# Hybrid decoder block: the last two experts' rows gathered, normed and stored by index

## Chip, core and metric

One core of one Trainium2 chip runs the whole block in one launch. The metric is device time in microseconds (us). TensorE is called PE, VectorE DVE, ScalarE ACT, GpSimd POOL; SP is the queue that issues plain DMAs.

## What is computed

One decoder layer on 1024 tokens of width 1024: a mixer of two attention groups, then a mixture of 32 experts with two experts for each token, then a last RMSNorm. Only the end matters here:

```python
g_sel = jnp.argmax(g_logits, axis=-1)                  # one group of 8 experts
top_v, top_i = lax.top_k(e_logits, 2)                  # two experts in it
w_top = jax.nn.softmax(top_v, axis=-1) * p_group[:, None]
a = jax.nn.silu(hg) * hu * comb[:, :, None]            # comb: w_top at the token's experts, else 0
y = jnp.einsum('nef,efd->nd', a, w_down)
x = x + gate_f * y
out = rms_norm(x, g_final)
```

## The kernel before

Up to the router all tokens are worked on in eight tiles of 128. The normed rows go to `h2d` and the residual rows to `x2d`, both in DRAM. `tab` holds for each expert a column of up to 128 token numbers; unused places hold numbers beyond the last token, which an indirect DMA skips.

The loop `for e in range(NE)` then takes one expert a turn, in a pipeline that spreads each expert over three turns. `gather(e)` (POOL, indirect DMA) brings the expert's token rows from `h2d` into `xg0` or `xg1`. `tokens_T` transposes them on PE, `tokens` splits them into a high and a low part, `gate_up` multiplies them with the gate and up weights (24 matmuls), `act` makes the gated product, `act_T` and `act_split` turn and split it, and `down_proj` multiplies it with the down weights (10 matmuls). `store` scales the result with the adaLN gate (`y = p * gf` on DVE), and `scatter` adds it by an indirect DMA with addition (POOL) to the rows of `x2d`. Each scatter waits for the one before it. `split_gu` and `split_dn` make the high and low parts of the weights on ACT and DVE, and SP loads weights into a ring of 29 buffers.

The last expert, 31, is not added in full by a scatter. `where(31)`, called in the turn of expert 29, builds one-hot matrices `ow` for the first four tiles, and two index columns, `late` and `early`. In the last turn `store(30)` scatters the rows of expert 30, `fetch(0)` to `fetch(3)` read back the first four tiles of `x2d` (SP), and after `down_proj(31)` `store(31)` scatters the rows of the later tiles alone; `fetch(4)` to `fetch(7)` wait for that. `add_last(i)` adds expert 31 to tile `i` of the first four by one-hot matmuls into `pf` and a DVE add into `xf`.

Each tile then goes through `square` (ACT, sum of squares; for tiles 0, 2 and 4 POOL multiplies the row with the final gain `bfin`), `mean` (DVE, then a square root on ACT), `roots` (four small DVE operations) and `last_norm` (ACT for tiles 0, 2, 4; DVE for the others), whose result SP stores with a plain DMA.

After that stands an `If` that is taken only when an expert has more than 128 tokens. In the runs shown it is not taken.

Order: instructions wrapped in `ko`, and all matmuls and transposes, keep their program order on their engine. The lines that the prediction's steps touch: L71 and L76 (all matmuls and transposes are recorded there), L1539 and L1540 (splits), L1584 and L1586 (`act`), L1599 to L1601 (`act_split`), L1617 (`scatter`), L1623 (`y`), L1641 to L1652 (`where`), L1674 (`fetch`), L1684 (`add_last`), L1689 and L1691 (`square`), L1694 and L1695 (`mean`), L1700 to L1703 (`roots`), L1709 to L1712 (`last_norm` and its store), L1761 (`bfin`), L1766 (table load), L1801 and L1940 (the `If` and the end of the program).

Of the kernel before, what the change touches and what calls it, by code (L numbers as in the profile page):

```python
# [19 lines left out]
NT = 8  # L20
# [18 lines left out]
def hymba_block(ctx: ExitStack, tc: tile.TileContext, x, c, w_ada, b_ada, g_mix, w_in, b_forget,  # L39
# [1510 lines left out]
    def split_dn(e):  # L1550

        hi, lo = fix("wd0h"), fix("wd0l")
        both(hi, lo, raw[e][4])
        DN[e] = hi, lo, raw[e][5]
# [41 lines left out]
    def act_split(e):  # L1596
        p = AS[e]
        hl, af = half("ahl", F32R, (128, 2, 128)), fix("af", F32, (128, 2, 128))[:, e % 2]
# [5 lines left out]
    def down_proj(e):  # L1604
# [15 lines left out]
    def store(e):  # L1620
# [3 lines left out]
        if e < NE - 1:  # L1624
            ko(scatter(e))
        else:
            d = ko(scatter(e, OW["late"]))
            for i in range(EARLY):
                tc.declare_no_dep(d.ins, XL[i].ins, reason="rows of later tiles")
# [7 lines left out]
    def where(e):  # L1637

        tn, fn = sm("tn", [128, EARLY + 1], bufs=1), sm("fn", [128, 2], bufs=1)
        ow = OW[e] = u("ow", F32R, (128, EARLY * 128))  # L1640
        ko(V.tensor_copy(tn[:, 0:1], tab[:, e:e + 1]))  # L1641
        for i in range(EARLY):
            ko(V.tensor_scalar(tn[:, i + 1:i + 2], tn[:, 0:1], -128.0 * i, None, op0=OP.add))
        for i in range(EARLY):
            ko(V.tensor_scalar(ow[:, i * 128:(i + 1) * 128], places, tn[:, i + 1:i + 2], None, op0=OP.is_equal))
        tn = tn[:, 0:1]

        for j, (name, op) in enumerate((("late", OP.is_lt), ("early", OP.is_ge))):
            ko(V.tensor_scalar(fn[:, j:j + 1], tn, EARLY * 128 - 0.5, float(FAR), op0=op, op1=OP.mult))
            ko(V.tensor_tensor(fn[:, j:j + 1], fn[:, j:j + 1], tn, op=OP.add))  # L1650
            OW[name] = sm(name, [128, 1], I32, bufs=1)
            ko(V.tensor_copy(OW[name], fn[:, j:j + 1]))  # L1652
# [15 lines left out]
    YS, OW, X2, XL, O = [{} for _ in range(5)]  # L1668
    EARLY = 4
    sqf, vf, yf, nf = (const.tile([128, NT], F32, name=n) for n in ("sqf", "vf", "yf", "nf"))  # L1670

    def fetch(i):
        X2[i] = u("xf")
        XL[i] = Q.dma_start(X2[i], x2d[i * 128:(i + 1) * 128])  # L1674

    def add_last(i):

        e = NE - 1
        p = ps2("pf")
        for hf in range(2):  # L1680
            sl = slice(hf * 512, (hf + 1) * 512)
            for a in range(2):
                mm(p[:, sl], OW[e][:, i * 128:(i + 1) * 128], YS[e][a][:, sl], start=(a == 0), stop=(a == 1))
        ko(V.tensor_tensor(X2[i], X2[i], p, op=OP.add))  # L1684
        square(i)
# [19 lines left out]
    POOL = (0, 2, 4)  # L1705

    def last_norm(i, pool=POOL):
# [4 lines left out]
        Q.dma_start(dap(out, i * 128 * D, [[D, 128], [1, D]]), O[i])  # L1712
# [6 lines left out]
    for e in range(NE):  # L1719
# [12 lines left out]
        if e == NE - 3:  # L1732
            where(NE - 1)
        if last:
            down_proj(e - 1)
# [5 lines left out]
        else:  # L1741
            store(e - 1)
            for i in range(EARLY):
                fetch(i)
            split_dn(e)
        act(e)
        if not last:
# [6 lines left out]
        else:  # L1754
            bfin = u("bfin")
            for hf in range(2):
                p = ps1("pbf")
# [187 lines left out]
```

## Time and profile before

| | us |
|---|---|
| three runs, median (lowest to highest) | 1187.88 (1185.55 to 1189.18) |
| profiled execution, its own time | 1188.36 |
| its span, first to last instruction | 1186.6 |
| PE busy in the span | 1059.7 |
| DVE busy | 873.4 |
| ACT busy | 708.1 |
| POOL busy | 251.7 |

Times in the rows are microseconds from the start of the span. A row of a timeline gives start, length, engine, line, operation, and output<-input; in brackets, how long the engine stood idle before it and what ended that. SPq and POOLq are the queues' own instructions. PEclk is the clock that PE was granted, as a share of the full one.

### The profile page before, as it was taken

To read this page: it belongs to the slowest core of one execution; us is meant where nothing else is said; L and a number is where in the kernel's file an instruction comes from. 1 tells how busy PE (TensorE), PEld (TensorE's weight loads), DVE (VectorE), ACT (ScalarE), POOL (GpSimd) and SP (SyncE) were. 2 spreads that over 40 slices of the span, in tenths; PEclk is the share of its full clock that TensorE was granted. 3 is DMA by queue.
4 is the path that set the end of the run, shared out by engine and by line. 5 is a ranking of instruction groups with operands and counts; after the bars stand their busy time and mean duration, and the time that the engine had idled before them with its cause. 6 is when DMAs were issued, how large, how long until landed. Compare 5 with 4: busy or idle time off the path is not lost.

```text
span 1186.6 us, 15360 instructions
## 1 busy us (share of the span) xinstructions
PE 1059.7 (89%) x4983; PEld 798.3 (67%) x4983; DVE 873.4 (74%) x1740; ACT 708.1 (60%) x1247; POOL 251.7 (21%) x240
## 2 busy tenths in 40 slices
PE   2899999999888999988989999975999999989882
PEld 2788998887665655655656678864777777766651
DVE  5846476768865689656478664796999999978856
ACT  7746578876657654644554631334777777756635
POOL 2110210000301111122212122552222223333213
PEclk9799999999889999999999999996999999989996
DMA  9500112323553343635336643766999999999946
GB/s 375 156 18 1 54 54 89 143 86 110 156 165 91 81 99 78 173 104 173 116 83 204 231 139 120 256 250 221 319 339 320 311 323 312 327 306 321 319 135 256
DMA packets 91415, 219.94 MB, mean 185 GB/s; under 512 B 30517, under 2 KB 40933, under 8 KB 91329
## 3 DMA queue, kind: packets, MB, share of 16 engines
q1 hardware_dynamic: 75520, 185.20, 46.3%
q0 software_dynamic: 15808, 33.69, 10.4%
q8 instruction: 42, 0.69, 0.2%
q14 instruction: 45, 0.36, 0.1%
HBM read 192.43 MB, written 42.99 MB: 198 GB/s over the span
## 4 chain that ended last, share of the span: by engine, by line
PE 60%; DVE 15%; DMA 14%; ACT 5%; issue 4%; SPq 1%; POOL 0%; DVEq 0%; ACTq 0%; POOLq 0%
PE pgu L71 10%; PE pp L305 9%; PE py L71 6%; PE pst L71 6%; PE po L71 5%; PE pout L71 5%; PE pvv L451 4%; DMA raw<-in_w_gate_dram 4%; DMA raw<-in_w_down_dram 3%; DMA qx<-mr 3%; PE pmax L71 3%; PE pxt L76 2%; PE pq L71 1%; PE pp L71 1%; DMA x<-in_x_dram 1%
## 5 line engine op out<-in xcount | busy, mean ns | idle before, releaser
L71 PE MATMUL po<-P,VT 128*128 128x512 f32 (+3 forms) x384 | 151.2, 507 | 0.3 <-ACT P L840 0.3
L840 ACT ACTIVATE P<-pst 128x512 f32<-128x512 f32 x192 | 90.8, 488 | 95.0 <-PE pst L71 93.1
L71 PE MATMUL pst<-qx,kx 128*128 128x512 f32 x192 | 97.2, 507 | 17.3 <-DMA qx<-mr 13.4
L1617 POOL DMA_INDIRECT x2d<-y,tab x31 | 58.5, 1887 | 200.1 <-DMA x2d<-y,tab 38.6
L805 DVE TENSOR_REDUCE mx<-pmax 128x1 f32<-128x128 f32 (+3 forms) x80 | 52.7, 673 | 48.0 <-PE pmax L71 47.8
L71 PEld LDWEIGHTS po<-P,VT 128*128 128x128 f32 x384 | 67.6, 199 | 18.6 <-issue 10.4
L71 PE MATMUL py<-raw,af 128*128 128x512 f32 x128 | 69.0, 621 | 11.4 <-DMA raw<-in_w_down_dram 11.3
L71 PE MATMUL pmax<-kx,qx 128*128 128x512 f32 (+1 forms) x192 | 70.4, 431 | 6.4 <-DMA kx<-KB 4.2
L71 PE MATMUL py<-wd0h,ahl 128*128 128x512 f32 x128 | 68.0, 531 | 2.4 <-ACT wd0h L1539 1.9
L71 PE MATMUL pst<-qy,ky 128*128 128x512 f32 x192 | 68.7, 358 | 0.0
L71 PEld LDWEIGHTS pst<-qx,kx 128*128 128x128 f32 x192 | 39.4, 205 | 39.3 <-issue 21.1
L802 DVE CUSTOM_DVE_ANT_0 mjunk<-pmax,madd 128x384 bf16<-128x384 f32 (+5 forms) x48 | 42.6, 888 | 21.9 <-PE pmax L71 21.7
L507 ACT ACTIVATE sjunk<-score,low,sga 128x768 bf16<-128x768 uint16 (+2 forms) x51 | 57.7, 1132 | 1.7 <-DVE low L537 0.8
L507 ACT ACTIVATE sjunk<-k,low 128x768 bf16<-128x768 uint16 (+2 forms) x48 | 49.9, 1039 | 13.3 <-DVE low L537 11.6
L402 DVE SCALAR_TENSOR_TENSOR score<-relu,iw,score 128x384 f32<-128x384 f32 (+5 forms) x42 | 41.0, 976 | 22.6 <-ACT relu L397 19.0
L71 PE MATMUL pout<-woh,oh 128*128 128x512 f32 x128 | 52.0, 406 | 2.4 <-DVE ssq L918 2.4
L71 PE MATMUL pout<-woh,ol 128*128 128x512 f32 x128 | 50.8, 397 | 0.0
L71 PE MATMUL pout<-wol,oh 128*128 128x512 f32 x128 | 50.5, 395 | 0.0
L305 PE MATMUL pp<-hh,wbl 128*128 128x512 f32 x128 | 49.8, 389 | 0.0
L305 PE MATMUL pp<-hl,wbh 128*128 128x512 f32 x128 | 49.8, 389 | 0.0
L305 PE MATMUL pp<-hh,wbh 128*128 128x512 f32 x128 | 49.8, 389 | 0.0
L1540 DVE TENSOR_TENSOR wgu2l<-raw,wgu2h 128x512 fp32r<-128x512 f32 x64 | 43.8, 684 | 8.0 <-ACT wgu2h L1539 8.0
(456 smaller groups left out, 3193.0 us busy)
## 6 DMA issues: line engine op xcount, KB each, us to landing
raw<-in_w_gate_dram SPq DMA_DIRECT2D x64, 512.0 KB
raw<-in_w_up_dram SPq DMA_DIRECT2D x64, 512.0 KB
raw<-in_w_down_dram SPq DMA_DIRECT2D x64, 512.0 KB
wada<-in_w_ada_dram POOLq DMA_DIRECT2D x32, 512.0 KB, 5.5
x<-in_x_dram SPq DMA_DIRECT2D x16, 512.0 KB
wada<-in_w_ada_dram SPq DMA_DIRECT2D x16, 512.0 KB
wbr<-in_w_in_dram SPq DMA_DIRECT2D x8, 512.0 KB
qy<-QB SPq DMA_DIRECT2D x16, 256.0 KB
```

Source lines behind the costliest of these rows:

```text
L71: i = tc.keep_in_program_order(T.matmul(*a, **k))
L76: i = tc.keep_in_program_order(T.transpose(*a))
L305: at["mm"] = (op or T.matmul)(p[:, :n], w(k, a), hT[b][k][:, n0:n0 + n], start=(i == 0), stop=(i == 23))
L402: last = V.scalar_tensor_tensor(score[i], r, wv, score[i], op0=OP.mult, op1=OP.add)
L451: at["mm"] = T.matmul(p[:, :ng], hT[a][k][:, t * 128:(t + 1) * 128], parts[k // kk][b][:, k % kk, :], start=(i == 0), stop=(i == 23))
L507: paced(S.activation(sjunk[:, :(i + 1) * 128], src, AF.Sign, bias=self.col(self.low, i), scale=scale, accum_out=self.col(self.cnt, i)))
L802: V.tensor_tensor_reduce(mjunk[:, :w_], p[:, :w_], madd[i], 1.0, NEG, OP.add, OP.max, accum_out=mx[0][:, i:i + 1])
L805: V.tensor_reduce(mx[0][:, i:i + 1], p[:, :w_], AX.X, OP.max)
L840: S.activation(P[hf, kb][0], p[:, :m], AF.Exp)
L1540: ko(V.tensor_tensor(lo, w, hi.bitcast(F32), op=OP.subtract))
L1617: return G.indirect_dma_start(out=x2d, out_offset=bass.IndirectOffsetOnAxis(ap=at_, axis=0), in_=y, in_offset=None, bounds_check=L - 1, oo ...
```

## The change

Experts 30 (`EA`) and 31 (`EB`) are no longer scattered into `x2d`. When the scatter of expert 29 has landed, `own_rows` gathers the residual rows of their tokens from `x2d` into `xg0` and `xg1`, and all eight tiles are fetched, without these two experts. The rows of expert 30 get its result, those of expert 31 get its own. A token that has both appears in both; `shares()` builds a 128x128 match `MT["m"]` between the two lists, and four more matmuls add expert 30's rows to those of 31, whose copy is the one stored. The gathered rows are treated as tiles 8 and 9 of the norm. Tiles 0 to 5 are stored plainly, also where a token's row lacks one of the two experts. Tiles 7 and 6 are stored by index without the tokens of either expert, then tile 9, and tile 8 without the tokens that tile 9 has. In the last turn, down projection of 30 moves behind gate and up of 31 and the gain; expert 31 gets buffers of its own for its down weights and its product. POOL multiplies for tile 6 too.

```diff
     def split_dn(e):
-        hi, lo = fix("wd0h"), fix("wd0l")
+        hi, lo = (fix(f"wd0{n}") if e < EB else u(f"wd1{n}", F32R) for n in "hl")
...
-            mm(p[:, sl], af, w1[:, sl], start=False, stop=True)
+            mm(p[:, sl], af, w1[:, sl], start=False, stop=(e != EB))
+        if e == EB:
+            for hf in range(2):
+                sl = slice(hf * 512, (hf + 1) * 512)
+                for k in range(2):
+                    mm(p[:, sl], MT["m"], YS[EA][k][:, sl], start=False, stop=(k == 1))
...
-        if e < NE - 1:
+        if e < EA:
             ko(scatter(e))
-        else:
-            d = ko(scatter(e, OW["late"]))
...
+        if e == EA:
             yh, yl = u("yh", F32R), u("yl", F32R)
-            for hf in range(2):
-                sl = slice(hf * 512, (hf + 1) * 512)
-                ko(S.activation(yh[:, sl], y[:, sl], AF.Copy))
-                ko(V.tensor_sub(yl[:, sl], y[:, sl], yh[:, sl].bitcast(F32)))
+            ko(S.activation(yh, p, AF.Copy))
+            ko(V.tensor_sub(yl, p, yh.bitcast(F32)))
             YS[e] = yh, yl
+        if e >= EA:
+            X2[NT + e - EA] = x = xgs[e % 2].bitcast(F32)
+            ko(V.tensor_tensor(x, x, y, op=OP.add))
+
+    def own_rows(e):
+        return ko(G.indirect_dma_start(out=xgs[e % 2], out_offset=None, in_=x2d,
+                                       in_offset=bass.IndirectOffsetOnAxis(ap=tab[:, e:e + 1], axis=0),
+                                       bounds_check=L - 1, oob_is_err=False))
+
+    def shares():
+        tn, fl = sm("tn", [128, 2], bufs=1), sm("fl", [128, 1 + NT], bufs=1)
+        ko(V.tensor_copy(tn, tab[:, EA:EA + 2]))
+        p = ps1("ptn")
+        mm(p[:, 0:128], tn[:, 1:2].to_broadcast([128, 128]), identf, start=True, stop=True)
+        MT["m"] = u("mt", F32R, (128, 128))
+        ko(V.tensor_scalar(MT["m"], p[:, 0:128], tn[:, 0:1], None, op0=OP.is_equal))
+        ko(V.tensor_reduce(fl[:, 0:1], MT["m"].bitcast(F32), AX.X, OP.max))
+        MT["a"] = sm("oa", [128, 1], I32, bufs=1)
+        ko(V.scalar_tensor_tensor(MT["a"], fl[:, 0:1], float(FAR), tn[:, 0:1], op0=OP.mult, op1=OP.add))
+        MT["d"] = sm("od", [128, NT], I32, bufs=1)
+        ko(V.tensor_tensor(fl[:, 1:], ohs[:, :, EA], ohs[:, :, EB], op=OP.add))
+        ko(V.tensor_scalar(fl[:, 1:], fl[:, 1:], 1.0, float(FAR), op0=OP.add, op1=OP.mult))
+        ko(V.tensor_tensor(MT["d"], fl[:, 1:], val[:, :, 0, 0], op=OP.add))
-    POOL = (0, 2, 4)
+    POOL, MASKED, outs = (0, 2, 4, 6), (6, 7), []
...
-        Q.dma_start(dap(out, i * 128 * D, [[D, 128], [1, D]]), O[i])
+        if i < NT and (i not in MASKED or pool == ()):
+            Q.dma_start(dap(out, i * 128 * D, [[D, 128], [1, D]]), O[i])
+
+    def put(i):
+        at_ = MT["d"][:, i:i + 1] if i < NT else MT["a"] if i == NT else tab[:, EB:NE]
+        d = ko(G.indirect_dma_start(out=dap(out, 0, [[D, L], [1, D]]),
+                                    out_offset=bass.IndirectOffsetOnAxis(ap=at_, axis=0),
+                                    in_=O[i], in_offset=None, bounds_check=L - 1, oob_is_err=False))
+        for o in outs:
+            tc.declare_no_dep(d.ins, o.ins, reason="each token's row once")
+        outs.append(d)
...
         if e == NE - 3:
-            where(NE - 1)
+            shares()
         if last:
-            down_proj(e - 1)
+            own_rows(EA)
+            own_rows(EB)
+            for i in range(NT):
+                fetch(i)
         gate_up(e)
...
         else:
+            bfin = final_gain()
+            split_dn(e)
+            act(e)
+            at["root"] = ko(S.preload_act_table_set("sqrt_and_others"))
         act_T(e)
...
+    act_split(EB)
+    down_proj(EA)
+    store(EA)
+    down_proj(EB)
+    square(0)
+    square(1)
+    mean(0, 2)
+    square(2)
+    square(3)
+    roots(0, 2)
+    last_norm(1)
+    square(NT)
+    store(EB)
+    mean(2, 2)
+    last_norm(0)
+    square(NT + 1)
+    mean(NT, 2)
+    square(4)
+    roots(2, 2)
+    last_norm(3)
+    roots(NT, 2)
+    square(5)
+    last_norm(NT + 1)
+    last_norm(2)
     mean(4, 2)
     square(6)
+    last_norm(NT)
+    roots(4, 2)
     square(7)
-    roots(4, 2)
+    mean(6, 2)
     last_norm(5)
-    mean(6, 2)
     last_norm(4)
     roots(6, 2)
+    last_norm(7)
     last_norm(6)
-    last_norm(7)
+    put(7)
+    put(6)
+    put(NT + 1)
+    put(NT)
```

`final_gain` holds the 16 matmuls and two copies that made `bfin` in the last turn before.

## Rows read from the trace of the kernel before

**Rows 1.** The page's second part: the span in 40 equal slices, mean busy share of the DMA engines in tenths.

```profile
DMA  9500112323553343635336643766999999999946
```

**Rows 2.** The chain of waits in order of time, from 1121 us: start, length, what.

```profile
1121.49 12.46 DMA raw<-in_w_down_dram
...
1140.10 3.14 PE py L71 x9
1143.24 5.49 PE pgu L71 x24
1148.73 1.99 PE pbf L71 x16
...
1151.56 5.02 PE py L71 x10
```

**Rows 3.** The timeline of SP's queue, the fetches of the eight tiles, merged.

```profile
1153.17 11.40 SPq L1674 DMA_DIRECT2D xf<-x2d  x8
```

**Rows 4.** The timeline of POOL: the last scatters, the multiplications with the final gain, and from the start of the expert loop the second of two gathers that followed each other.

```profile
811.34 1.42 POOL L1530 DMA_INDIRECT xg<-h2d,tab  x1 [0.30 <-issue]
...
1139.87 1.61 POOL L1617 DMA_INDIRECT x2d<-y,tab  x1 [8.31 <-DMA x2d<-y,tab]
1146.79 1.54 POOL L1617 DMA_INDIRECT x2d<-y,tab  x1 [5.31 <-DMA x2d<-y,tab]
...
1163.44 2.38 POOL L1691 TENSOR_TENSOR of<-xf,bfin 128x1024 f32<-128x1024 f32 x1 [3.80 <-ACT of L1689]
1166.29 2.36 POOL L1691 TENSOR_TENSOR of<-xf,bfin 128x1024 f32<-128x1024 f32 x1 [0.48 <-ACT of L1689]
1171.80 3.18 POOL L1691 TENSOR_TENSOR of<-xf,bfin 128x1024 f32<-128x1024 f32 x1 [3.15 <-ACT of L1689]
```

**Rows 5.** Views of one tile. From issue to landing, first of the scatters of experts 29 and 30 (1139 to 1147 us), second of that of 31 (1157 to 1164 us); then the last six gathers (1050 us to the end): duration on POOL in ns (min/median/max), and issue to landing in us.

```profile
DMA to landing us min/median/max: 6.2/6.3/6.3
...
DMA to landing us min/median/max: 4.7/4.7/4.7
...
L1530 POOL DMA_INDIRECT xg<-h2d,tab x6: 1037/1039/1224, 1056.4 to 1110.8; - x6
...
DMA to landing us min/median/max: 8.2/8.5/9.3
```

**Rows 6.** Busy time of each engine in two stretches, with PE's granted clock, the DMA engines' share and GB/s at the end.

```profile
1152.20:1155.60 3.40, 3.40 (x8) 2.03 (x7) 0.00 (x0) 0.00 (x0) 0.00 (x0) 0.50 0.42 140
1178.00:1181.00 3.00, 0.00 (x0) 0.00 (x0) 2.89 (x5) 0.79 (x1) 0.00 (x0) 0.50 0.91 356
```

**Rows 7.** The timelines of PE and DVE in the turn of expert 29, and PE's transposes of expert 30's product.

```profile
1115.29 0.47 PE L71 MATMUL pgu<-wgu0h,xh 128*128 128x512 f32 x1
...
1118.85 0.14 DVE L1641 CAST tn<-tab 128x1 f32<-128x1 int32 x1
...
1123.95 1.12 PE L71 MATMUL py<-raw,af 128*128 128x512 f32 x2 [1.38 <-DMA raw<-in_w_down_dram]
...
1136.51 0.38 PE L76 MATMUL pat<-identf,at 128*128 128x128 f32 x2
```

**Rows 8.** The timelines of ACT and DVE in the last turn: split of the down weights of 31, gated product, second copy of the gain, table load.

```profile
1142.42 1.06 ACT L1539 ACTIVATE wd0h<-raw 128x1024 fp32r<-128x1024 f32 x1 [3.63 <-PE py L71]
1144.42 1.21 DVE L1540 TENSOR_TENSOR wd0l<-raw,wd0h 128x1024 fp32r<-128x1024 f32 x1
1149.18 0.48 DVE L1586 SCALAR_TENSOR_TENSOR at<-pgu,tabf,sg 128x256 f32<-128x256 f32 x1 [3.55 <-ACT sg L1584]
1150.74 0.60 ACT L1761 ACTIVATE bfin<-pbf 128x512 f32<-128x512 f32 x1 [0.30 <-PE pbf L71]
1159.02 1.28 ACT L1766 ACT_TABLE_LOAD   x1
```

**Rows 9.** ACT's instructions by line from 1157 us: busy us, mean ns of one, then idle time before them.

```profile
L1689 ACT ACTIVATE of<-xf 128x1024 f32<-128x1024 f32 x8 | 8.4, 1050 | 2.4 <-DVE xf L1684 2.4
```

**Rows 10.** The timeline of DVE in the norm.

```profile
1166.33 1.22 DVE L1684 TENSOR_TENSOR xf<-xf,pf 128x1024 f32<-128x1024 f32 x1
...
1167.79 0.88 DVE L1701 TENSOR_TENSOR nf<-vf,yf 128x2 f32<-128x2 f32 x1
...
1171.50 1.28 DVE L1711 SCALAR_TENSOR_TENSOR of<-xf,yf,bfin 128x1024 f32<-128x1024 f32 x1
1172.79 2.21 DVE L1694 TENSOR_SCALAR vf<-sqf 128x2 f32<-128x2 f32 x1
...
1175.47 0.16 DVE L1701 TENSOR_TENSOR nf<-vf,yf 128x2 f32<-128x2 f32 x1
```

**Rows 11.** The end: SP's last store, then the queues' own instructions at the `If` and at the program's end: durations in ns (min/median/max), first and last start in us. SP's eight waits at L1801 are for the eight stores.

```profile
1181.08 0.33 SPq L1712 DMA_DIRECT2D out_dram<-of  x1
...
L1801 SPq EVENT_SEMAPHORE  x8: 17/17/17, 1181.7 to 1184.9; - x8
L1801 POOLq EVENT_SEMAPHORE  x5: 17/43/43, 1176.5 to 1176.9; - x5
...
L1801 POOLq INC_SWDGE_SEM  x1: 935/935/935, 1176.9 to 1176.9; - x1
...
L1940 POOLq EVENT_SEMAPHORE  x4: 17/17/17, 1185.8 to 1186.5; - x4
L1940 POOLq DRAIN  x3: 46/109/3092, 1177.9 to 1186.3; - x3
```

More of the change, by code (lines that the diff above doesn't have):

```diff
@@ L1597, in act_split @@
         p = AS[e]
-        hl, af = half("ahl", F32R, (128, 2, 128)), fix("af", F32, (128, 2, 128))[:, e % 2]
+        hl = half("ahl", F32R, (128, 2, 128)) if e < EB else u("ahl", F32R, (128, 2, 128))
+        af = fix("af", F32, (128, 2, 128))[:, e % 2]
         ko(S.activation(hl[:, 0], p[:, 0:128], AF.Copy))
@@ L1635, in store @@
             YS[e] = yh, yl
[L1637 to L1652, printed above, removed]
+        if e >= EA:
+            X2[NT + e - EA] = x = xgs[e % 2].bitcast(F32)
+            ko(V.tensor_tensor(x, x, y, op=OP.add))
@@ L1666, in totals @@
         entries()
-    YS, OW, X2, XL, O = [{} for _ in range(5)]
-    EARLY = 4
-    sqf, vf, yf, nf = (const.tile([128, NT], F32, name=n) for n in ("sqf", "vf", "yf", "nf"))
+    YS, MT, X2, O = [{} for _ in range(4)]
+    EA, EB = NE - 2, NE - 1
+    sqf, vf, yf, nf = (const.tile([128, NT + 2], F32, name=n) for n in ("sqf", "vf", "yf", "nf"))
     def fetch(i):
         X2[i] = u("xf")
[L1674 to L1685, printed above, removed]
+        Q.dma_start(X2[i], x2d[i * 128:(i + 1) * 128])
     def square(i, pool=None):
@@ L1711, in last_norm, with final_gain @@
             ko(V.scalar_tensor_tensor(O[i], X2[i], yf[:, i:i + 1], bfin, op0=OP.mult, op1=OP.mult))
-        Q.dma_start(dap(out, i * 128 * D, [[D, 128], [1, D]]), O[i])
+        if i < NT and (i not in MASKED or pool == ()):
[8 more added lines that the diff above has]
+        outs.append(d)
+    def final_gain():
+        b = u("bfin")
+        for hf in range(2):
+            p = ps1("pbf")
+            for k in range(4):
+                i = 24 + hf * 4 + k
+                mm(p[:, k * 128:(k + 1) * 128], identf[0:32, i:i + 1].to_broadcast([32, 128]), vt, start=True, stop=True)
+            ko(S.activation(b[:, hf * 512:(hf + 1) * 512], p, AF.Copy))
+        return b
     for j in range(4):
@@ L1740, in hymba_block @@
                 refill(1)
[L1741 to L1747, printed above, removed]
+            act(e)
             tokens(e + 1)
@@ L1754, in hymba_block @@
         else:
[L1755 to L1786 removed]
+            bfin = final_gain()
+            split_dn(e)
+            act(e)
+            at["root"] = ko(S.preload_act_table_set("sqrt_and_others"))
+        act_T(e)
+    act_split(EB)
[12 more added lines that the diff above has]
+    mean(2, 2)
+    last_norm(0)
+    square(NT + 1)
[6 more added lines that the diff above has]
+    last_norm(NT + 1)
+    last_norm(2)
     mean(4, 2)
     square(6)
+    last_norm(NT)
+    roots(4, 2)
     square(7)
[L1790 removed]
+    mean(6, 2)
     last_norm(5)
[L1792 removed]
     last_norm(4)
     roots(6, 2)
+    last_norm(7)
     last_norm(6)
[L1796 removed]
+    put(7)
+    put(6)
+    put(NT + 1)
+    put(NT)
     NO = 2 * L // 128 - 1
@@ L1905, in hymba_block @@
                                  in_=y, in_offset=None, bounds_check=L - 1, oob_is_err=False, compute_op=OP.add)
-        scatter(NE - 1, OW["early"])
+        scatter(EA, MT["a"])
+        scatter(EB)
         for i in range(NT):
```

26 lines of the change are left out of this document (removed).

## Prediction

> **What bounds the kernel now.** I read the slices first, then the chain of waits, then the tail engine by engine. The slices show the DMA engines at nine tenths in the ten slices up to the 38th, and at four and six in the last two [rows 1]: the later expert loop is bound by its weights, and the diff touches almost only what comes after the last of them, so the loop's length is not in question. In the chain, DMA of weights is the last cause until 1134; then PE, ACT and DVE take turns to the end [rows 2]. The reader should see three stretches there. From 1134 to 1156.6, PE: down projection of expert 30, gate and up of 31, the 16 small matmuls of the gain, down projection of 31. From 1156.6 to 1163, the last expert's rows are put in by one-hot matmuls. From 1163 to 1181, DVE's normalisation with ACT and POOL beside it, and the last store. Fetches of the sum start late, at 1153.17 [rows 3], when the scatter of expert 30 has landed.
>
> The profiled execution took 1188.36 us, 1.76 more than its span; the median of the three runs is 0.48 below it. Each time below is on the span's scale; 1.3 added gives the median's.
>
> **What goes, and what that is worth.** Two scatters go: that of 30, 1.54 us of POOL and landed 6.3 after issue, and that of 31, landed 4.7 after issue [rows 4, 5]. The fetches then wait for the scatter of 29 alone: issued 1139.87, landed 6.2 later, 1146.1 instead of 1153.1. Seven microseconds of fetching come earlier. Also gone are 16 one-hot matmuls, four adds into xf and the copies of y in two parts. In their place stand four matmuls with the 128x128 match, one pair of copies, and two adds into gathered rows. Tile 0 is now needed at 1156 and tile 7 near 1176 (below), and eight tiles of 512 KB, at the 356 GB/s of the loaded stretch at the end [rows 6], are in by about 1161. They are hidden, and so is their gain, except for the start of the normalisation.
>
> **Start of the normalisation.** (a) The new match is built where the one-hots were, but it sends a matmul through PE ahead of gate and up of expert 29, and this matmul waits for a DVE cast. PE began that gate and up at 1115.29; the cast of the same kind stood at 1118.85 [rows 7]. Queued behind it is all of PE's work: 4.1 us late (the cast, a hop and the matmul itself included), of which the wait for weights at 1123.95 swallows 1.4 [rows 7]. DVE's own part is about even, eight small operations for fourteen. I take 2.6, with ends 0 (were the cast early) and 4.1. (b) Down projection of 30 no longer stands ahead of gate and up of 31, so these begin after the transposes that ended at 1136.89 [rows 7]: 1136.9 + 2.6 = 1139.5. Then in a line, as the diff orders them: 24 matmuls 5.7 (5.49 in the chain, and the end of the last one), gain 2.0 [rows 2], second gain copy 0.6, split of the down weights 1.06 on ACT and 1.21 on DVE, the gated product 0.48 [rows 8], transposes 0.38 [rows 7]: 1151.0. The table load (1.28 [rows 8]) lies beside the DVE half of the split and the product; without that cover it costs up to 1.3. Then ten matmuls of expert 30: 3.14 in the chain at the full clock, 5.02 where 0.50 was granted in most of the stretch after PE's pauses [rows 2, 6]; PE now pauses some 3 us ahead of them, and I take 4.0: 1155.0. Copy of its result and square of tile 0, 1.05 each [rows 9]: at 1157.2 POOL begins its first multiplication. Before, it began at 1163.44 [rows 4]. So six of the seven microseconds survive to here.
>
> **The normalisation itself, now of ten tiles.** DVE and POOL keep each other out. While POOL multiplied (1166.29 to 1168.65), a two-input DVE operation of two columns that takes 0.16 elsewhere took 0.88 and ended with it; a norm on DVE at 1171.50 stretched POOL's from 2.36 to 3.18, and the next DVE operation took 2.21, to POOL's end [rows 4, 10]. The add into xf, which reads PSUM, ran at 1.22 beside POOL [rows 10]. So the stage is near a sum: before, from 1163.44, 7.1 of POOL, 6.4 for five norms of 1.28, 2.9 of adds and 4.2 for five sets of five small operations of 0.17 make 20.6 [rows 4, 10], against 17.6 measured to 1181.06, since the PSUM adds overlap. After: POOL four times 2.37, 9.5; six norms 7.7; two adds and y of 31, 3.7; five sets 4.2: 25.1. Only y of 31 reads PSUM, so less overlaps; ACT's root, its scale of tile 0 and the square of the second gathered tile stand between two DVE steps, and add some 2. I take 25, with ends 21.4 (25.1 x 17.6/20.6) and 27: last norm at 1182.2, 1.1 later than before. ACT is no bound: ten squares of 1.05 [rows 9], four scales of about the same and five small roots: 16 us.
>
> The two adds into gathered rows have no row of their own. By the PSUM add they would pass beside POOL, and the stage would be up to 2.4 shorter; by the norm, which like them has both inputs in SBUF, they wait, and I take that. The Trainium skill, page "SBUF — State Buffer", section "Who interferes with whom", has it so: a DVE instruction with two SBUF inputs contends with a GpSimd one that reads SBUF, and the second to issue blocks fully. By that rule 25 stands, without it 22.6.
>
> Gathers of the own rows follow the scatter on POOL. They landed 8.2 to 9.3 after issue under load [rows 5]; issued at 1147 and 1148 they are there by 1155 to 1158, when their adds are due. I cost them at nothing; a later one is a rival.
>
> **The stores by index.** Six tiles are stored plainly, four by POOL at the very end. Each of these names all of the output, so the first waits for every plain store, and the three others are queued behind it on POOL. The last two plain stores are ready one norm and one set of small operations ahead of the last norm: 1180.1, the second issued at 1180.5. A plain store issued at 1181.08 landed at 1184.9 [rows 11], so 1184.3; POOL took 0.7 from a landing to its next issue (1146.1 to 1146.79 [rows 4]): first store by index at 1185.0. One costs between 1.04 (gather) and 1.61 (scatter without load), with 0.3 between two [rows 4, 5]; nothing of this trace stores by index without adding. Four of 1.3 and three gaps: 6.1, with ends 5.1 and 7.3: 1191.1. The landing came 3.1 after the end of issue for the smaller scatter (4.7 less 1.54), 4.7 for the larger; writes without the addition are nearer the smaller: 1194.2.
>
> The Trainium skill, page "DMA: Bandwidth & Descriptors", section "Anatomy of one DMA — SWDGE (gpsimd) path", fits such a transfer as 2.0 us + bytes/436 GB/s. For 512 KB that is an estimate of 3.2 from issue; the sum would be 1.2 less.
>
> **The close.** Before, the program ended 1.7 after the last landing, by SP. POOL had long closed: its waits, an increment of the indirect queues' semaphores (0.94) and a drain of 3.09, from 1176.5 to 1181 [rows 11]. Now these waits are for the stores by index, so 0.4 + 0.94 + 3.09 come after the landing, and the common end of 0.8 (1185.8 to 1186.6 [rows 11]): 5.2, with 1.7 as the low end if the drain only happened to be long. I take 5.0: 1199.2. On the median's scale 1200.5.
>
> **Rivals.** First, the overlap is as good as before and the close is cheap: stage at 2.2 a tile, 22, last norm 1179.2; plain stores landed and POOL awake at 1182.0; four stores of 1.04 with gaps, 5.1, landing 3.1, close 1.7: 1191.9, or 1193. For it: the old stage's 17.6 against 20.6; against: fewer PSUM adds. Second, on the other side: DVE and POOL don't bind, ACT's 16 us do, from 1156.1. Last norm at 1173.5 at best; every term behind it is 17.0 together, so 1190.5, or 1191.8, and 1188.5 with the cheap close. It is faster than now by 0.3% only from a last norm at 1166 (1169.3 with the cheap close); that needs the matmul's stall gone too, and the adds beside POOL. Against it: the 0.88 and 2.21 us rows. Third, the change doesn't do what it says: the gathered rows come last instead of apart, since their packets share the engines with eight fetches. With a landing 12 after issue and the scatter itself late, their add, to which the first mean is tied on DVE, comes some 3 us later: 1203.5.
>
> **How the numbers follow.** The forecast has 0.65, its own range 1194 to 1206; the first rival 0.17, the second 0.10, the third 0.08. The likeliest is 1200.5. The terms with ends (2.6, 4.0, 25, 6.1, 3.1, 5.0) together allow some 6 below and 5 above; the first rival reaches 1193 and lower with a smaller stall: 1190 to 1206. A measurement of this kernel can tell 0.3%, 3.6 us, from no change: 1184.3 and 1191.4 are the bounds. Half of the second rival, 0.05, is faster; its other half, a quarter of the first and the forecast's low tail are within, 0.13; 0.82 is slower.
>
> **What would show it.** PE still for 4 us before gate and up of expert 29; fetches at 1147; last norm between 1179 and 1184; POOL without a break from some 1185 in four issues; an increment and a drain of 3 us after the last landing, as the last things on POOL. Wrong would be: stores by index that start before the plain ones have landed, DVE passing beside POOL, or a close of under 2 us.

## The result, and the profile after

The changed kernel took 1199.34 us (median of four runs, 1198.99 to 1201.08), the kernel before 1188.07 beside it: ratio 1.0101, 95% interval 1.0082 to 1.012. It is slower by some 11 us; a later session with six runs gave 1.0127 (1.0094 to 1.016), some 15. The rows below are of one execution of 1201.08 us, span 1199.3.

The expert loop's length scatters by several us between executions of one kernel: in one session the kernel before ran from 1179.71 to 1192.93. So I also measure from a mark inside the program: the first of SP's last five loads of down weights. From it to the end of the span is called **the stretch** here. By the timelines of SP's queue, first before, where the stretch is 1186.6 - 1121.5 = 65.1 us, then after:

```profile
1121.49 7.78 SPq L1453 DMA_DIRECT2D raw<-in_w_down_dram  x5
```

```profile
1119.62 7.83 SPq L1453 DMA_DIRECT2D raw<-in_w_down_dram  x5
...
1147.95 3.81 SPq L1685 DMA_DIRECT2D xf<-x2d  x8
...
1181.02 0.81 SPq L1713 DMA_DIRECT2D out_dram<-of  x2
```

The mark comes 1.9 sooner by chance, and the stretch is 1199.3 - 1119.6 = 79.7: 14.6 longer. The fetches are issued together at 1147.95, as wanted, instead of in two halves from 1153.17 [rows 3].

PE's timeline in the turn of expert 29, to be held against [rows 7]: the match's matmul stands ahead of gate and up, and PE stands still for it.

```profile
1117.23 0.49 PE L71 MATMUL ptn<-identf,tn 128*128 128x128 f32 x2 [3.54 <-DVE tn L1652]
1117.47 0.48 PE L71 MATMUL pgu<-wgu0h,xh 128*128 128x512 f32 x1
```

POOL's timeline from the gathers on, to be held against [rows 4]. It has two gathers in place of two scatters, a fourth multiplication, and then the four stores by index.

```profile
1148.67 1.26 POOL L1644 DMA_INDIRECT xg<-x2d,tab  x1 [5.40 <-issue]
1150.24 1.04 POOL L1644 DMA_INDIRECT xg<-x2d,tab  x1 [0.30 <-PE pat L76]
1158.02 2.36 POOL L1691 TENSOR_TENSOR of<-xf,bfin 128x1024 f32<-128x1024 f32 x1 [6.75 <-DMA xf<-x2d]
1162.89 3.20 POOL L1691 TENSOR_TENSOR of<-xf,bfin 128x1024 f32<-128x1024 f32 x1 [2.52 <-ACT of L1689]
1171.12 2.83 POOL L1691 TENSOR_TENSOR of<-xf,bfin 128x1024 f32<-128x1024 f32 x1 [5.03 <-ACT of L1689]
1177.12 2.34 POOL L1691 TENSOR_TENSOR of<-xf,bfin 128x1024 f32<-128x1024 f32 x1 [3.16 <-ACT of L1689]
1186.18 1.03 POOL L1718 DMA_INDIRECT out_dram<-of,od  x1 [6.72 <-SPq L1823]
1187.52 1.00 POOL L1718 DMA_INDIRECT out_dram<-of,od  x1 [0.30 <-issue]
1188.82 0.97 POOL L1718 DMA_INDIRECT out_dram<-of,tab  x1 [0.30 <-issue]
1190.10 0.98 POOL L1718 DMA_INDIRECT out_dram<-of,oa  x1 [0.30 <-issue]
```

DVE's timeline in the norm, to be held against [rows 10]. Four instructions are long: an add into gathered rows that takes 3.38, the other 2.12, and two operations of two columns at 2.12 and 2.22. Each lies over one of POOL's multiplications: the small ones end with it, the adds 1.1 after it.

```profile
1154.62 1.22 DVE L1630 TENSOR_TENSOR y<-py,gf 128x1024 f32<-128x1024 f32 x1 [3.84 <-PE py L71]
1156.93 1.22 DVE L1636 TENSOR_TENSOR yl<-py,yh 128x1024 fp32r<-128x1024 f32 x1 [1.09 <-ACT yh L1635]
1158.08 3.38 DVE L1640 TENSOR_TENSOR xg<-xg,y 128x1024 f32<-128x1024 f32 x1
...
1165.05 2.12 DVE L1640 TENSOR_TENSOR xg<-xg,y 128x1024 f32<-128x1024 f32 x1
...
1169.60 0.17 DVE L1694 TENSOR_SCALAR vf<-sqf 128x2 f32<-128x2 f32 x1 [2.35 <-ACT of L1689]
...
1171.85 2.12 DVE L1701 TENSOR_TENSOR nf<-vf,yf 128x2 f32<-128x2 f32 x1
...
1177.26 2.22 DVE L1702 SCALAR_TENSOR_TENSOR nf<-nf,yf 128x2 f32<-128x2 f32 x1
...
1181.69 1.28 DVE L1711 SCALAR_TENSOR_TENSOR of<-xf,yf,bfin 128x1024 f32<-128x1024 f32 x1
```

The queues' own instructions at the `If` and at the program's end, to be held against [rows 11] (durations in ns, first and last start in us). SP's eight waits at L1823 include those for the plain stores; the last one passes at 1185.5, and 0.7 later POOL issues its first store by index. POOL's increment and its long drain, which before ran from 1176.9 to 1181 beside the last norms, now stand behind the last landing.

```profile
L1823 SPq EVENT_SEMAPHORE  x8: 17/17/17, 1182.1 to 1185.5; - x8
...
L1823 POOLq INC_SWDGE_SEM  x1: 1020/1020/1020, 1194.0 to 1194.0; - x1
...
L1963 POOLq DRAIN  x3: 46/109/3418, 1195.1 to 1199.0; - x3
```

The kernel before ends its last norm, by DVE's timeline, with

```profile
1178.58 2.48 DVE L1711 SCALAR_TENSOR_TENSOR of<-xf,yf,bfin 128x1024 f32<-128x1024 f32 x2
```

The 14.6 us in three pieces:

| piece | before | after | difference |
|---|---|---|---|
| mark to POOL's first multiplication | 42.0 | 38.4 | -3.6 |
| from there to the end of the last norm | 17.6 | 25.0 | +7.3 |
| from there to the end of the span | 5.5 | 16.3 | +10.8 |

So the norm starts 3.6 us sooner. Scatters and one-hot products that are gone can't be credited with that: with the last turn reordered and nothing else (below) it starts 3.7 sooner. With PE's stall mended (below) it starts 6.7 to 7.2 sooner, so if the reorder is worth the same there, their removal brings some 3, and the stall takes that back. The gain is paid for twice: by two more tiles in a norm in which DVE and POOL exclude each other, and by a serial end on POOL.

### The profile page after: what moved, and what is told of

Read it like the earlier page. It is cut to its first block, busy times and chain, and to the rows that moved or that the text cites. A ratio compares the mean times of both kernels' runs of the same rounds, so it can differ in the third digit from the quotient of the medians.

```text
span 1199.3 us, 15326 instructions
## 1 busy us (share of the span) xinstructions
PE 1051.5 (88%) x4962; PEld 794.3 (66%) x4973; DVE 876.3 (73%) x1730; ACT 710.4 (59%) x1251; POOL 258.7 (22%) x245
## 5 line engine op out<-in xcount | busy, mean ns | idle before, releaser
L71 PE MATMUL po<-P,VT 128*128 128x512 f32 (+3 forms) x384 | 148.0, 498 | 1.1 <-ACT P L840 0.3
L71 PEld LDWEIGHTS pst<-qx,kx 128*128 128x128 f32 x192 | 38.4, 200 | 40.5 <-issue 16.0
L71 PE MATMUL py<-wd0h,ahl 128*128 128x512 f32 x124 | 65.1, 525 | 0.0
L1530 POOL DMA_INDIRECT xg<-h2d,tab x32 | 39.6, 1239 | 48.9 <-PE pxt L76 34.2
```

The source lines that it names most:

```text
L71: i = tc.keep_in_program_order(T.matmul(*a, **k))
L1530: return ko(G.indirect_dma_start(out=XG[e], out_offset=None, in_=h2d, in_offset=bass.IndirectOffsetOnAxis(ap=tab[:, e:e + 1], axis=0), bou ...
```

## The experiments

Each run below lists the ratio to the kernel before of its own session with its 95% interval, and the stretch of its profiled execution. Stretches are of one execution each. From the mark to POOL's first multiplication five of them are of the same program (the changed kernel twice, and the runs with none, one and two stores by index), and that piece takes 38.4, 37.9, 39.3, 39.4 and 39.1. So a difference of 1.5 between two stretches decides nothing, and where less matters I count from that multiplication on.

**The stall of PE.** The cast that the match's matmul waits for is moved seven turns ahead.

```diff
+    def early_cast():
+        MT["t"] = sm("tn", [128, 2], bufs=1)
+        ko(V.tensor_copy(MT["t"], tab[:, EA:EA + 2]))
     def shares():
-        tn, fl = sm("tn", [128, 2], bufs=1), sm("fl", [128, 1 + NT], bufs=1)
-        ko(V.tensor_copy(tn, tab[:, EA:EA + 2]))
+        tn, fl = MT["t"], sm("fl", [128, 1 + NT], bufs=1)
...
             totals()
+            early_cast()
```

> The changed kernel, with the DVE cast that the match's matmul waits for moved from the turn of expert 29 to that of expert 22. Theory: PE's 3.5 us stall ahead of gate and up of expert 29 comes one for one at the start of the norm, since the scatter of 29 and the gathers move with it: 1196 us, 3 less than the changed kernel. Rival, that the weights' DMA or the landing of the gathered rows sets the start anyway: 1198.5 to 1199.5.

Measured: 1198.46, ratio 1.0098 (1.0068 to 1.0128); stretch 76.5. By the time alone it could not be told from the changed kernel; its stretch was 3.2 shorter, and gate and up of 31 began 15.2 after the mark instead of 18.8. The changed kernel and this one were run once more on one chip:

> The changed kernel once more, unaltered, beside the next run on the same chip. Its profiled execution grew by 14.6 us between the first of the last five loads and the end, its median of four runs by 11.3 only. Theory (the length of the loop scatters by several us between executions, four runs are few, and the stretch after the loop is the measure): the stretch is again 79 to 80 us, and the ratio over more runs is 1.0115 to 1.0125, that is 13.5 to 15 us. Rival (the loop itself is shorter in the changed kernel): the ratio stays at 1.0095 to 1.0105 with the same stretch.

> The changed kernel with the cast of the match early, once more, beside the changed kernel itself on the same chip. Theory (PE's stall of 3.5 us reaches the end): 3.2 us below the changed kernel, a stretch of 76 to 77 us after the loop. Rival (the loop takes it back): the medians within 1 us of each other.

Measured: the changed kernel 1203.89 (six runs, 1200.0 to 1204.96), ratio 1.0127 (1.0094 to 1.016), stretch 79.1; with the early cast 1198.75 (1194.65 to 1202.53), ratio 1.0096 (1.0062 to 1.0131), stretch 76.1. The stall reaches the end with about 3 us in both pairs of stretches, and the loop doesn't take it back. At gate and up of 31 the second pair differs less, 17.3 after the mark against 15.2 (why, below). The medians say 5.1, in the same direction and with the loop's scatter in them. 1.0127 fits the longer stretch and not the rival of a shorter loop; but the two sessions' intervals overlap, so that the rival isn't out by the times alone.

**DVE against POOL.** All norms are left to DVE.

```diff
-    POOL, MASKED, outs = (0, 2, 4, 6), (6, 7), []
+    POOL, MASKED, outs = (-1,), (6, 7), []
```

> The changed kernel with POOL's four multiplications and ACT's four scales replaced by four more norms on DVE (1.28 us each). Theory, that DVE and POOL keep each other out: 9.5 us of POOL go and 5.1 of DVE come, so the norm is 4.4 us shorter, 1195 us. Rival, that POOL works beside DVE: the norm grows by up to 5 us, 1199 to 1204.

Measured: 1195.64, ratio 1.007 (1.0047 to 1.0093); stretch 73.6, 6.1 less than the changed kernel. Its rows, first of DVE's timeline (the two adds, and the last norms), then of POOL's (its first store by index), then of SP's waits:

```profile
1155.41 1.21 DVE L1640 TENSOR_TENSOR xg<-xg,y 128x1024 f32<-128x1024 f32 x1
...
1160.22 1.22 DVE L1640 TENSOR_TENSOR xg<-xg,y 128x1024 f32<-128x1024 f32 x1
...
1170.57 0.17 DVE L1694 TENSOR_SCALAR vf<-sqf 128x2 f32<-128x2 f32 x1 [0.50 <-ACT of L1689]
...
1173.84 2.48 DVE L1711 SCALAR_TENSOR_TENSOR of<-xf,yf,bfin 128x1024 f32<-128x1024 f32 x2
```

```profile
1176.73 1.01 POOL L1718 DMA_INDIRECT out_dram<-of,od  x1 [28.94 <-DVEq L1823]
```

```profile
L1823 SPq EVENT_SEMAPHORE  x8: 17/17/17, 1173.7 to 1176.0; - x8
```

The adds take 1.2 where they took 3.38 and 2.12, and no small operation is long. So four multiplications on POOL saved DVE 5.1 (four norms of 1.28) and cost it 7.1 (2.2 + 0.9 + 2.0 + 2.1), 2.0 net. The last norm ends 60.0 after the mark instead of 63.4, and 24.4 after the start of `y` of expert 30 instead of 28.4: 4.0 less, where 4.4 were expected. The half of it that the sum doesn't have is DVE's wait for ACT: 2.35 for the square of the second gathered tile in the changed kernel, 0.50 as the longest in the norm here. One of ACT's scales (1.13), which go with POOL's multiplications, stood ahead of that square, so this run doesn't part POOL from ACT altogether. The other 2.8 of the stretch come behind the last norm: DVE now finishes the last two plain tiles well ahead of the two masked ones, the plain stores have landed by 1176.0, when the last norm is just ending, and POOL's first store waits for nothing more. Behind POOL's multiplication and ACT's scale they were ready at 1181, and their landing was waited for. The rows agree with the Trainium skill, page "SBUF — State Buffer", section "Who interferes with whom", weighed in the prediction: an add with two SBUF inputs is held for as long as POOL reads SBUF. Its 25 for the norm is what the changed kernel took.

**The stores by index, taken out.** All eight tiles are stored plainly, nothing by index; the last two experts' rows are left out of the output.

```diff
-    POOL, MASKED, outs = (0, 2, 4, 6), (6, 7), []
+    POOL, MASKED, outs = (0, 2, 4, 6), (), []
...
-    put(7)
-    put(6)
-    put(NT + 1)
-    put(NT)
```

> The changed kernel without the four stores by index; all eight tiles are stored plainly. Left out: the last two experts' rows never reach the output. Theory, that these stores and POOL's close after them are the loss (8.6 us from the last plain landing to the last landing, then 5.3 instead of 1.7): the last plain store lands 1.2 us later than before, and the end comes 1.7 after that, 1188 us, 11 less. Rival, that the loss sits in the longer norm of ten tiles: 1196 or more.

Measured: 1193.19, ratio 1.0051 (1.003 to 1.0071); stretch 71.5, 8.2 less than the changed kernel, and 9.1 less from POOL's first multiplication on (32.2 for 41.3), where 11 were expected. The queues' rows at the end, then a window of DMA share and GB/s (columns as in [rows 6]):

```profile
L1819 SPq EVENT_SEMAPHORE  x8: 17/17/17, 1183.9 to 1188.2; - x8
L1819 POOLq INC_SWDGE_SEM  x1: 940/940/940, 1180.7 to 1180.7; - x1
...
L1959 POOLq DRAIN  x3: 46/109/3092, 1181.6 to 1189.6; - x3
```

```profile
1181.50:1184.50 3.00, 0.00 (x0) 0.00 (x0) 1.19 (x1) 1.11 (x1) 0.00 (x0) 0.50 1.00 399
```

The close is cheap again: the last landing at 1188.2, the end 1.7 later, and POOL's drain of 3.09 from 1181.6 is hidden, as before [rows 11]. What the expectation missed is in the first row. With eight plain stores, four of them issued from 1180.7 to 1183.5, the last lands at 1188.2, 30.4 after POOL's first multiplication, where the changed kernel's six had landed at 27.5: 3.0 later. Four stores of 512 KB that come within 3 us queue for the DMA engines, which are busy throughout that window at 399 GB/s; the changed kernel's plain queue is spared two of them.

**One store by index.** The changed kernel with one put of the four.

```diff
-    put(7)
-    put(6)
-    put(NT + 1)
     put(NT)
```

> The changed kernel with one store by index in place of four (that of expert 30's rows); the rows of tiles 6 and 7 and of expert 31's tokens are left out. Theory (the four are a plain line on POOL, each 1.0 us and a gap of 0.3, behind fixed costs: the wait for the last plain store, one landing, the close): the program ends 3.8 us sooner after the first store by index than with four; median about 1195.5; after the last landing still 5.4 to the end. Rival (the landings or the close grow with the number of stores, so that the slope is steeper): 5 or more us less, 1194 or under, with a close under 5. Rival (the line is hidden beside the landing): 1198 or more.

Measured: 1198.0, ratio 1.0096 (1.0073 to 1.012); stretch 76.0, 3.7 less. The time can't decide: it fits the last rival beside the first session's 1.0101, and the theory beside the later 1.0127. The trace does. The queues' rows at the end:

```profile
L1820 SPq EVENT_SEMAPHORE  x8: 17/17/17, 1182.1 to 1185.5; - x8
L1820 POOLq INC_SWDGE_SEM  x1: 960/960/960, 1189.6 to 1189.6; - x1
...
L1960 POOLq DRAIN  x3: 46/109/3173, 1190.6 to 1194.4; - x3
```

The indirect queue from 1185.9 to 1190 (packets, MB, share of the engines):

```profile
q0 software_dynamic: 144, 0.23, 14.6%
```

From the issue of the first store by index (1186.17) to the end of the span (1194.6) it takes 8.4; with four it took 13.1 (1186.18 to 1199.3). Three stores are 4.7, or 1.6 each: 1.3 for issue and gap, the rest in a longer landing and a longer close. That is between the theory (3.8) and the steeper rival (5 and more): the line on POOL isn't hidden, and each store adds a little behind it. The close has a fixed part of about 5 us: 0.96 of increment, 3.17 of drain, 0.8 at the end. Counted from the last plain landing to the end of the span: 1.7 without stores by index (1188.2 to 1189.9, above), 9.1 with one (1185.5 to 1194.6), 13.8 with four. The first costs 7.4, each further one 1.6.

**Two stores by index, eight plain ones.** A way to spare two of the four.

```diff
-    POOL, MASKED, outs = (0, 2, 4, 6), (6, 7), []
+    POOL, MASKED, outs = (0, 2, 4, 6), (), []
...
-    put(7)
-    put(6)
     put(NT + 1)
     put(NT)
```

> The changed kernel with all eight tiles stored plainly, and only the two gathered tiles by index (two in place of four). A plain count (two stores by index fewer) gives 2.6 us less: 1196.7. Theory (the first store by index waits for the landing of every plain one, and with eight plain stores, four of them in the last 2.5 us, that landing comes some 4 us later after the loop's end, as in the run without stores by index): 4.0 more and 2.6 less, 1200.7.

Measured: 1201.27, ratio 1.0114 (1.0091 to 1.0138); stretch 80.4. The plain count falls. SP's waits and POOL's first store:

```profile
L1821 SPq EVENT_SEMAPHORE  x8: 17/17/17, 1185.0 to 1189.3; - x8
```

```profile
1190.10 1.02 POOL L1718 DMA_INDIRECT out_dram<-of,tab  x1 [9.81 <-SPq L1821]
```

The last plain store lands 30.4 after POOL's first multiplication (1189.3 - 1158.9), 3.0 later than with six, as in the run without stores by index, and from there to the end it takes 10.9 instead of 13.8. The one eats the other: from that multiplication to the end it takes 41.3 in both kernels.

**Order of two readers of one PSUM tile.** In the changed kernel ACT's copy `yh` and DVE's product `y` both read `py`, and ACT began 1.26 after DVE, when that had ended. Here the copy stands first.

```diff
+        if e == EA:
+            yh, yl = u("yh", F32R), u("yl", F32R)
+            ko(S.activation(yh, p, AF.Copy))
         ko(V.tensor_tensor(y, p, gf, op=OP.mult))
         if e < EA:
             ko(scatter(e))
         if e == EA:
-            yh, yl = u("yh", F32R), u("yl", F32R)
-            ko(S.activation(yh, p, AF.Copy))
```

> The changed kernel with ACT's copy yh of expert 30's result put ahead of DVE's product y in the program; both read the same PSUM tile, and before this ACT began only when DVE had ended. Theory (the two readers of one PSUM tile are put in program order): now ACT begins with the end of the matmuls, 1.1 us sooner, and DVE waits for it; the squares and POOL's first multiplication come 1.1 us sooner, the add into the gathered rows no later, since POOL holds it anyway; median about 1198.3. Rival (ACT waited for something else that ended with y): ACT begins no sooner and 1199.3 stays.

Measured: 1200.89, ratio 1.0114 (1.0092 to 1.0136); stretch 79.2. The timelines (the last of expert 30's ten matmuls on PE, ACT, DVE, and POOL's first multiplication):

```profile
1154.54 1.02 PE L71 MATMUL py<-raw,af 128*128 128x512 f32 x2
```

```profile
1155.59 1.02 ACT L1632 ACTIVATE yh<-py 128x1024 fp32r<-128x1024 f32 x1 [3.32 <-PE py L71]
```

```profile
1156.65 1.23 DVE L1633 TENSOR_TENSOR y<-py,gf 128x1024 f32<-128x1024 f32 x1 [4.69 <-ACT yh L1632]
...
1158.92 2.27 DVE L1641 TENSOR_TENSOR xg<-xg,y 128x1024 f32<-128x1024 f32 x1
```

```profile
1157.74 2.38 POOL L1692 TENSOR_TENSOR of<-xf,bfin 128x1024 f32<-128x1024 f32 x1 [5.27 <-ACT of L1690]
```

The wait changes sides: whichever reader stands first, the other starts behind it. From the end of the matmuls to POOL's first multiplication it takes 2.2 now (1155.56 to 1157.74) instead of 3.4, so the theory's 1.1 is there. The add, which POOL holds until that multiplication is done, ends 5.6 after the matmuls instead of 6.9. Whether any of this reaches the end is not shown: the stretch is 0.5 shorter, which decides nothing, and the median lies above the forecast of 1198.3 and above the rival's 1199.3. The rows agree with the Trainium skill, page "PSUM — Partial Sum Buffer", section "PSUM bank collisions raise a hardware error": two engines may not access one bank at once (within the same 32 partitions), reads included, and the program has to order them.

**The reorder alone.** The kernel before, with only its last turn reordered (scatters, one-hot products and plain stores as before). As in the change, gate and up of 31 run ahead of down projection of 30; that stands ahead of `act` of 31 here, and the gain behind `act_split`, so the order isn't the change's in every place.

```diff
-        hi, lo = fix("wd0h"), fix("wd0l")
+        hi, lo = (fix(f"wd0{n}") if e < NE - 1 else u(f"wd1{n}", F32R) for n in "hl")
...
-        if last:
-            down_proj(e - 1)
         gate_up(e)
...
-            store(e - 1)
-            for i in range(EARLY):
-                fetch(i)
             split_dn(e)
+            down_proj(e - 1)
         act(e)
...
+            act_T(e)
+            store(e - 1)
+            for i in range(EARLY):
+                fetch(i)
+            act_split(e)
             bfin = u("bfin")
...
-        act_T(e)
-    act_split(NE - 1)
+        if not last:
+            act_T(e)
```

> The kernel before with one part of the change alone: expert 31 has down weights and a product in buffers of its own, gate and up of 31 run ahead of down projection of 30, and the gain's matmuls fill the wait for the split of the product. No gathered rows and no stores by index. Theory: PE's last product comes 5 us earlier, the one-hot adds 4.4 earlier (then bound by the fetch of tile 0 at 1156.4), and the norm moves with them: 1183.7 us. Rival, that the scatter and fetch chain holds the norm: 1187 to 1188.

Measured: 1182.52 (12 runs, 1180.82 to 1187.94), ratio 0.9965 (0.9945 to 0.9985); stretch 62.2, 3.0 less than before. It is faster than both kernels. 4.4 were expected; DVE's timeline shows what took the rest: the first adds, with their products ready, wait for the fetch, and then the third does. Last, POOL's first multiplication, 38.3 after this run's mark at 1119.34.

```profile
1155.12 2.50 DVE L1685 TENSOR_TENSOR xf<-xf,pf 128x1024 f32<-128x1024 f32 x2 [3.04 <-DMA xf<-x2d]
...
1158.69 1.22 DVE L1685 TENSOR_TENSOR xf<-xf,pf 128x1024 f32<-128x1024 f32 x1 [0.98 <-DMA xf<-x2d]
```

```profile
1157.60 2.37 POOL L1692 TENSOR_TENSOR of<-xf,bfin 128x1024 f32<-128x1024 f32 x1 [4.10 <-ACT of L1690]
```

**POOL's share on that version.** None of three multiplications, and two of three.

```diff
-    POOL = (0, 2, 4)
+    POOL = (-1,)
```

> The kernel before with the last turn reordered (as in the run named so), and without POOL's three multiplications; DVE does all eight norms. Theory (DVE and POOL exclude each other, and what it costs is the sum of the stretched DVE operations): DVE loses 2.9 us of stretching (0.9 and 2.0) and gains three norms of 1.28, so 0.9 more than with POOL: about 1183.4. Rival (a norm without POOL gains some 5 us as it did in the changed kernel): 1177.5 to 1179.

Measured: 1183.17, ratio 0.9975 (0.9957 to 0.9992); stretch 62.0. No gain of 5 us here, and no loss of 0.9 either: from DVE's first add to the end of its last norm it takes 20.4, against 20.8 with three multiplications.

```diff
-    POOL = (0, 2, 4)
+    POOL = (0, 2)
```

> The kernel before with the last turn reordered, and POOL multiplying for tiles 0 and 2 alone (its multiplication for tile 4, beside which DVE lost 2.05 us, is left to DVE's norm). Theory (what a multiplication on POOL costs or brings is read from what DVE does beside it: the first ran beside adds that read PSUM and cost DVE nothing, the second cost 0.9, the third 2.0, and each saves a norm of 1.28): 0.8 less than with three and 0.6 less than with none: 61.4 from the first of the last five loads to the end, about 1182. Rival (the gaps in which DVE waits for ACT take it up): the same as either, 62.0 to 62.2.

Measured: 1183.93, ratio 0.9977 (0.9953 to 1.0); stretch 62.0. The norm did become shorter: from DVE's first add it takes 19.6, against 20.8 with three multiplications and 20.4 with none. But from the last norm to the last landing it now takes 4.8 instead of 3.9 and 4.3; why isn't shown, since in all three the last two norms stand one behind the other on DVE and their stores 1.2 apart. The theory holds for DVE, not for the end. The three variants can't be told apart by time.

**All that could be mended.** The changed kernel with the early cast, POOL off and the copy ahead together.

> The changed kernel with three edits of the earlier runs together: the cast of the match early, no multiplication on POOL, the copy yh ahead of y. Theory (stall, exclusion and stores by index are separate terms that stand one behind the other): 3.2 and 6.2 less after the loop than the changed kernel, and about nothing for the copy, since no POOL stands behind it: 70.3 us from the first of the last five loads to the end, against 65.1 for the kernel before; so 0.4% slower than before, near 1192 where before is at 1187. Rival (with the rest earlier, the gathered rows land last and take part of it back): 71.5 or more. Rival (the terms overlapped, and together bring more than each alone): under 69, the time of before.

Measured: 1191.82 (12 runs), ratio 1.004 (1.0018 to 1.0063); stretch 69.2. The terms add, a little better than the theory's 70.3, and the version stays 4 us longer than the kernel before. In it POOL's first store by index comes 0.4 after the last norm, so no plain landing is left to wait for; what is left behind the last norm is 13.5 us, all of it index stores, their landing and the close.

## Why the prediction was right

The direction, the place and the mechanism hold, and the median fell 1.2 below the forecast of 1200.5. Part of that closeness is luck: in the profiled execution the loop ended 1.9 early, and the stretch was 79.7 where the prediction's steps made 77.7; in the later session, with a stretch of 79.1, the median was 1203.89, 3.4 above the forecast. Of its own steps five were too short, two too long:

| step | predicted | measured | why |
|---|---|---|---|
| mark to gate and up of 31 | 18.0 | 18.8 | PE 4.0 late; 1.4 swallowed at the weights, but 24 matmuls at reduced clock |
| from there to the end of expert 30's ten matmuls | 15.5 | 16.1 | PE at half clock in the first half of them |
| to POOL's first multiplication | 2.2 | 3.4 | the copy waited 1.1 for the other reader of `py` |
| norm of ten tiles | 25 | 24.95 | |
| last norm to first store by index | 2.8 | 3.2 | second plain store 1.5 ahead of the last norm, not 1.7, and landed 4.0 after issue, not 3.8 |
| four stores by index | 6.1 | 4.9 | 1.0 each and 0.3 between, not 1.3 |
| landing | 3.1 | 2.9 | |
| close | 5.0 | 5.3 | increment 1.02, drain 3.42 |

**Start of the norm.** (a) came out at 3.6 in this execution (18.8 after the mark against 15.2 with the early cast), where the sum has 2.6. The two numbers that made the 2.6 were about right: gate and up of 29 began 4.0 late, and the wait for weights of 1.38 at 1123.95 before [rows 7] is gone, while with the cast early it stands (1.10 and 1.09 in the two runs). What the sum lacked is PE's clock behind the stall. These are the windows of gate and up of 29 (columns as in [rows 6]): before; in the changed kernel, behind its pause of 3.54; and in the changed kernel run again, behind a pause of 3.29.

```profile
1115.30:1120.80 5.50, 5.50 (x27) 4.53 (x25) 5.21 (x19) 3.32 (x7) 2.55 (x1) 1.00 0.90 345
```

```profile
1117.50:1124.60 7.10, 7.10 (x26) 5.66 (x26) 3.90 (x11) 2.83 (x5) 1.05 (x1) 0.76 0.97 335
```

```profile
1121.00:1126.60 5.60, 5.60 (x27) 4.59 (x27) 3.83 (x11) 2.83 (x5) 1.09 (x1) 1.00 0.93 294
```

The 24 matmuls took 7.15 in the second, 5.55 in the two others. The 0.76 is a mean: one matmul takes 0.63 from 1118.7 to 1121.7, at the half clock, and some 0.4 ahead of that and behind it, at the full one. Where the clock stayed up, gate and up of 31 began 2.1 later than with the early cast, near the 2.6; where it fell, 1.6 came on top. The ten matmuls of expert 30 took 4.8 for the 4.0 of the sum, also behind a pause of PE (3.29); their reduced clock is seen in the windows of that stretch. With the last turn reordered alone PE doesn't pause ahead of them, and they took 3.3.

```profile
1149.80:1152.20 2.40, 2.40 (x8) 1.59 (x6) 0.29 (x1) 0.55 (x2) 1.17 (x2) 0.50 1.01 387
1152.20:1154.60 2.40, 2.40 (x8) 1.33 (x7) 0.00 (x0) 0.00 (x0) 0.00 (x0) 0.87 1.03 401
```

The wait of one reader of `py` for the other was not in the sum at all; with it POOL's first multiplication came 3.4 after the matmuls, without it 2.2, as predicted.

**The norm.** 25 held, and for the reason given: the adds with both inputs in SBUF stood behind POOL (3.38 and 2.12 against 1.2 with POOL off), and DVE waited 2.35 for ACT's square of the second gathered tile, where I had put "some 2". That ACT doesn't bind is shown by the same row: it is the one long wait for ACT in the stage.

**Gathers.** This trace doesn't give their landing; in the changed kernel run again, and in the runs with the early cast and with one store by index, they landed 8.1 to 9.4 after issue. By that they were there before 1160, and neither add has a wait for them in its row (1158.08 and 1165.05). So the third rival is out. The second (ACT as the bound, DVE and POOL side by side) is out by the long adds; the first (good overlap, cheap close) by a norm of 24.95 and a close of 5.3.

**The end.** The wait of the first store for every plain landing, four issues in a line on POOL, and an increment and drain behind the last landing are in the trace as described, and the runs with none, one, two and four stores show their price. The single store landed 3.2 after issue; of the four the trace gives one landing, 3.5 after issue, and the last, issued at 1190.10, had landed by the increment at 1194.0, 3.9 after. The 3.2 that the prediction sets beside its sum, from the Trainium skill's fit (page "DMA: Bandwidth & Descriptors", section "Anatomy of one DMA — SWDGE (gpsimd) path"), agrees by luck: it was reckoned for 512 KB, and the single store, of one expert's tokens, moved 0.23 MB. For that the fit's estimate is 2.5, 0.7 short of the measured time.

What stays open: whether the changed design could gain without any indirect DMA at the end. The run without stores by index has neither them nor the serial scatters, but it leaves rows out, still has the stall and POOL's multiplications, and stays 6.4 above the stretch before; no run took all three away. Nor was it tried to let the stores of tiles 7 and 6 go ahead of the plain stores' landing: no plain store writes to their rows, and both were ready at the end of the last norm, 3.2 ahead of the first store by index.

## What to carry to other kernels

An indirect store at the very end is priced by more than its issue: as written here it waits for all plain stores to the same tensor, its successors queue behind it, and it moves the indirect queue's increment and drain from under the last work to behind it; here 7.4 us for the first and 1.6 for each other. Before POOL is given a share of an elementwise stage, hold its saving against what DVE instructions that read SBUF lose beside it (the adds with two SBUF inputs 2.2 and 0.9, small operations of two columns up to 2.1); products and adds that read PSUM lost nothing here (1.22 beside POOL). A pause that one engine's queue gets from a wait can cost more than itself: PE's 24 matmuls behind one took 1.6 more in one execution, at a lower granted clock, and nothing more in another. And a change of several parts should be split: here the reorder alone made the kernel 0.35% faster, and was hidden under some 17 us of net losses from the rest (14.6 and 3.0 in the stretch).

## What the runs showed that was not expected

- The close on POOL grows with the number of indirect stores: increment 0.94, 0.96, 0.98 and 1.02, drain 3.09, 3.17, 3.26 and 3.42 with none, one, two and four stores by index at the end. So the drain has a length of its own (3.09 when all had long landed), and some 0.08 comes with each store.
- A store by index without addition issues in 0.97 to 1.03, as the shorter gathers do (1.04; the longest took 2.1), less than the scatters with addition (1.5 to 2.7 in these traces).
- The same program's piece from the mark to POOL's first multiplication took 37.9 to 39.4 in five executions. PE's clock behind the stall has a part in it: gate and up of 29 took 5.55 at 1.00 in the shortest, 7.15 at 0.76 in the one shown, and 8.1 at 0.67 in the longest, the run with one store by index.
